# V of the attention layer computed by a Strassen product at the end of the gMLP layer

## The chip, the cores and the metric

The kernel runs on one core of a Trainium2 chip. A core has TensorE (PE, matrix products; its weight loads are shown as PEld), VectorE (DVE), ScalarE (ACT), GpSimd (POOL) and SyncE (SP), which issues the transfers between DRAM and the on-chip memory. Each engine takes its instructions in order. The metric is the device time of one execution in microseconds; of several runs the median is given.

## The reference, cut to what matters

Two layers act on x, 2048 tokens of width 1024, in float32. Layer A is a gated MLP over groups of 128 tokens. Layer B is attention in chunks of 64 tokens, each over itself and the 8 chunks before; its K and V come from the output x1 of layer A.

```
h  = rms_norm(x, a_norm_g)
u, v, z = split(h @ w_in, 3)                  # 1024 -> 3 x 2048
x1 = x + (gelu(u) * mix(layer_norm(gelu(v))) * silu(z)) @ w_out
k, v = split(rms_norm(x1, g_kv) @ w_kv, 2)    # 1024 -> 2 x 1024, the V of this case
q, z = split(rms_norm(x1, b_norm_g) @ w_qz, 2)
o  = softmax(q k^T + rel_bias over 9 chunks) v, 16 heads of 64
out = rms_norm(x1 + (o * silu(z)) @ wb_out, final_norm_g)
```

V is a product of 2048 x 1024 (normalized rows of x1) and 1024 x 1024 (the second half of w_kv, its rows scaled by g_kv). It is needed head by head, beside Q, K and the gate z.

## The kernel before, in words

Every float32 product is made of three products of rounded halves: a number is split into hi (a copy in the rounded type fp32r) and lo (the rest), and mm3 (lines 96 to 98) adds hi·hi, hi·lo and lo·hi in PSUM. A split is a copy on ACT and a subtraction on DVE (lines 255 and 258, in layer B 176 and 177).

**Layer A** is one sequence of steps. Six input stages n = 0 to 5 and the output stage "o" are each a product by Strassen's scheme in Winograd's form: both operands are cut in 2 x 2 blocks, and seven products of sums of blocks take the place of eight. The seven are the phases, in the order PH = (1, 2, 6, 5, 7, 4, 3), and each has 8 steps j, one for a pair of row blocks of 128 tokens. In stage o a step is 24 matmuls of 128 x 512 (Po). For each phase the weights' sums T are loaded, combined on GpSimd in pieces of 256 columns (line 264) and split. The row operands of stage o are So: prep_out loads blocks of the gated rows from DRAM (A<-ytd, line 796, a ring of four buffers; the first blocks stay in sc), adds or subtracts them (line 821 and its neighbours on DVE, line 264 on GpSimd in s2_of) and splits them. evict adds each PSUM result to the partial sums of its block, and done_out adds the residual x (xr) and stores x1 into x1d.

run_steps runs act of step s (its matmuls) and before it prep of step s + 3 (LOOK = 3); at(s, f) puts other work at a step, among it the weight loads and load_scaled. load_scaled loads 512 KB of weights (line 161), scales them by g on GpSimd (line 165) and stores the scaled ones for later tiles (line 168). All transfers are issued by SP in the order in which they stand. The framework's scheduler orders the instructions of each engine within what the data allow; that order is then fixed.

Steps of stage o are counted from nin, its first step. Weights for layer B are scaled at nin + 26, 28 and 30 (K, Q, Z of the first pair of heads) and nin + 32 and 34 (V of the first two pairs, raw_bv). At nin + 51 the rows of the first token tile are begun.

**Layer B** takes four tiles t of 512 tokens, each with eight pairs of heads p. norm_transpose (lines 118 to 157) makes the operands of a tile once: it loads x1 rows (bx_b), normalizes them (statistics on DVE, a power on GpSimd, line 115, a scaling on DVE), transposes them on TensorE (tr_b, line 145), and splits the result into hh_b and hl_b (lines 150 and 151). The first tile's is done at the end of stage o, the others' inside the projections.

The attention of a pair (t, p) has 8 slots: score (matmul s, the row maximum and bias on DVE at line 1067, the exponential on ACT at 1074, the scaling on GpSimd at 1078), flip (transposes tp, copies pt at 1098 to 1102) and value (pv, lines 1118 to 1125). Between them a generator yields the projections of the next pair as filler: Q and K with 8 yields each, V for two pairs at once with 16 yields of 6 matmuls of 128 x 256 (vp, proj_v), and the gate with 8 yields. Gates of two pairs are computed in the even pair. share fixes how many yields go into a pair, 32 before. proj_v splits V (lines 965 and 966) and stores it (vhd), since the next tile needs it as its previous 8 chunks. The output projection b4 (bo) stands between tiles.

Of the kernel before, what the change touches and what calls it, by code (L numbers as in the profile page):

```python
# [33 lines left out]
def trunk_kernel(  # L34
# [83 lines left out]
    def norm_transpose(name, src, wide, pool, tag, bufs):  # L118

        th = sh.tile([P, KD, T], F32R, tag="hh", name=f"hh_{name}")  # L120
        tl = sh.tile([P, KD, T], F32R, tag="hl", name=f"hl_{name}")

        xs = {}

        def norm(b):
            xt = pool.tile([P, D], F32, tag=tag, name=f"bx_{name}_{b}", bufs=bufs)
            nc.sync.dma_start(xt[:], src(b))
            r = inv_rms(xt, f"{name}_{b}")
            nc.vector.tensor_scalar(xt[:], xt[:], r[:], None, op0=ALU.mult)
            xs[b] = xt  # L130

        def block(b):
            if b not in xs:
                norm(b)
            xt = xs[b]
            if wide:
                pt = ptr.tile([P, KD, P], F32, tag="tr", name=f"tr_{name}_{b}")
                half = [pt[:, 0:4, :], pt[:, 4:8, :]]
            else:
                half = [  # L140
                    pmm.tile([P, 4, P], F32, tag="mm", name=f"tr_{name}_{b}_{h}")[:]
                    for h in range(2)
                ]
            for k in range(KD):
                tpose(half[k // 4][:, k % 4, :], xt[:, k * P : (k + 1) * P], ident[:])
            for h in range(2):
                ks = slice(h * 4, h * 4 + 4)
                oh = th[:, ks, b * P : (b + 1) * P]
                ol = tl[:, ks, b * P : (b + 1) * P]
                nc.scalar.copy(oh, half[h])  # L150
                nc.vector.tensor_tensor(ol, half[h], oh.bitcast(F32), op=ALU.subtract)
            if b + 2 < TB:
                norm(b + 2)

        for b in range(2):
            norm(b)
        return [(th[:, k, :], tl[:, k, :]) for k in range(KD)], block
# [29 lines left out]
    def v_source(t, pp, half):  # L187
        name = f"bv{int(t)}_{pp}_{half}"
        if t:
            return wvv[pp][:, half, :], name  # L190
        g = kg[:, half * 4 : half * 4 + 4, :]
        return w_vv[pp, :, half, :], name, g, wvv[pp][:, half, :]

    xT = {}

    def b1(t, *where):
        xT[t], block = norm_transpose(
            f"b{t}", lambda b: x1d[t][b * P : (b + 1) * P, :], t == 0, *where
        )
        return block  # L200
# [8 lines left out]
    with ExitStack() as actx:  # L209
# [598 lines left out]
        def prep_out(ph, j):  # L808
# [10 lines left out]
            elif ph == 7:  # L819
                v, b = y_load(0, 0, j, ph), y_load(1, 0, j, ph)  # L820
                tv(v, v, b, op=sub)
# [566 lines left out]
```

## Time and profile before

| | us |
|---|---|
| three runs, lowest, median, highest | 2738.63, 2742.27, 2744.74 |
| the profiled execution, its span | 2739.6 |
| layer A before stage o | 0 to 1069.9 |
| stage o | 1069.9 to 1404.1 |
| layer B | 1404.4 to the end |

The profiled execution's own time is its span; the medians of the runs lie 2.7 us above it. In the profile's tables, a row of a stretch of time gives for each engine its busy time and the count of instructions (x), then the clock granted to TensorE (1.00 is full) and the DMA share and rate. In a row of the timeline stand start, duration, engine, line, operation and tiles; a bracket at its end tells how long the engine had been idle, and what it waited for. A group's row gives, after the bar, total busy time and the mean in ns of one, and then the idle time before its members. Names lose their numbers: Po stands for all Po tiles.

### The profile page before, as it was taken

The page shows a single profiled execution, that of the slowest core. Times are in us where ns is not written, and L with a number is a line of the kernel's source. Part 1 is how long each engine was busy: PE and PEld are TensorE (multiplying, and loading weights), DVE is VectorE, ACT ScalarE, POOL GpSimd, SP SyncE. Part 2 cuts the span into 40 slices and gives each one's busy share as a digit, 9 for nine tenths or more (in the row PEclk, how much of TensorE's full clock was granted, in tenths as well). Part 3 has the DMA queues.
Part 4 walks back from the last instruction along what each step waited for, and adds up shares of the span by engine and source line. Part 5 has one row for each costly group of instructions (what it writes and reads, how often), then busy time and mean ns, then how long its engine had stood idle before and what let it go on. Part 6 is the DMA issues. An engine that isn't in the chain of part 4 may idle for free.

```text
span 2739.6 us, 40113 instructions
## 1 busy us (share of the span) xinstructions
PE 2673.4 (98%) x14176; PEld 2271.7 (83%) x14176; DVE 1918.0 (70%) x3211; ACT 1275.2 (47%) x2244; POOL 756.7 (28%) x951
## 2 busy tenths in 40 slices
PE   8899999999999999999999999999999999999997
PEld 6788888888888888777878888899988999889996
DVE  5556566756667566566767666877788777787777
ACT  5423243443433434232235554566655666556663
POOL 4611133241232423733024530211112112021111
PEclk9999999999999999999999999999999999999998
DMA  7799998986877868758766665455455444453331
GB/s 277 265 326 330 325 332 308 321 306 235 312 262 256 306 234 320 258 198 282 255 212 233 214 198 167 161 154 153 150 169 166 150 152 150 153 164 115 118 111 70
DMA packets 209191, 607.17 MB, mean 222 GB/s; under 512 B 24288, under 2 KB 24288, under 8 KB 208992
## 3 DMA queue, kind: packets, MB, share of 16 engines
q1 hardware_dynamic: 208992, 604.62, 64.3%
q8 instruction: 113, 1.85, 0.3%
q14 instruction: 86, 0.70, 0.1%
HBM read 466.11 MB, written 127.93 MB: 217 GB/s over the span
## 4 chain that ended last, share of the span: by engine, by line
PE 44%; DVE 7%; DMA 5%; POOL 2%; issue 1%; ACT 1%; SPq 0%; DVEq 0%; POOLq 0%; ACTq 0%
PE pj L96 5%; PE pj L97 5%; PE pj L98 5%; PE s L1059 4%; PE tp L1098 4%; PE pv L1125 4%; PE vp L98 2%; PE vp L96 2%; PE vp L97 2%; DMA A<-ytd 2%; PE bo L96 2%; PE bo L98 2%; PE bo L97 2%; PE Po L98 1%; PE Po L97 1%
## 5 line engine op out<-in xcount | busy, mean ns | idle before, releaser
L96 PE MATMUL P<-T,S 128*128 128x512 f32 x1248 | 496.3, 398 | 2.5 <-ACT S L255 2.1
L98 PE MATMUL P<-T,S 128*128 128x512 f32 x1248 | 490.6, 393 | 0.0
L97 PE MATMUL P<-T,S 128*128 128x512 f32 x1248 | 489.3, 392 | 1.1 <-DVE T L258 1.1
L1078 POOL TENSOR_SCALAR pr<-pr,sl 128x640 f32<-128x640 f32 (+4 forms) x256 | 200.2, 782 | 766.7 <-DVE sl L1077 678.6
L1074 ACT ACTIVATE pr<-pr,nm 128x640 f32<-128x640 f32 (+4 forms) x256 | 195.6, 764 | 274.8 <-DVE nm L1067 274.4
L96 PE MATMUL pj<-hh_b,wh_b 128*128 128x512 f32 x768 | 311.9, 406 | 0.7 <-ACT hh_b L150 0.7
L97 PE MATMUL pj<-hl_b,wh_b 128*128 128x512 f32 x768 | 302.6, 394 | 0.0
L98 PE MATMUL pj<-hh_b,wl_b 128*128 128x512 f32 x768 | 301.4, 392 | 0.0
L98 PEld LDWEIGHTS P<-T,S 128*128 128x128 f32 x1248 | 235.4, 189 | 50.1
L96 PEld LDWEIGHTS P<-T,S 128*128 128x128 f32 x1248 | 235.7, 189 | 45.1 <-ACT S L255 2.3
L97 PEld LDWEIGHTS P<-T,S 128*128 128x128 f32 x1248 | 235.7, 189 | 44.0 <-DVE T L258 1.3
L1102 DVE TENSOR_TENSOR pt<-tp,pt 128x640 fp32r<-128x640 f32 (+4 forms) x256 | 188.8, 737 | 59.0 <-ACT pt L1101 56.4
L1067 DVE CUSTOM_DVE_ANT_0 pr<-s,bias 128x640 f32<-128x640 f32 (+4 forms) x256 | 188.2, 735 | 44.6 <-PE s L1059 40.3
L98 PEld LDWEIGHTS pj<-hh_b,wl_b 128*128 128x128 f32 x768 | 144.5, 188 | 33.3
L1098 PE MATMUL tp<-ident,pr 128*128 128x128 f32 x1120 | 165.0, 273 | 4.6 <-DVE pt L1102 3.9
L1101 ACT CAST pt<-tp 128x640 fp32r<-128x640 f32 (+4 forms) x256 | 159.1, 621 | 21.1 <-PE tp L1098 15.5
L1098 PEld LDWEIGHTS tp<-ident,pr 128*128 128x128 f32 x1120 | 134.8, 140 | 32.3 <-issue 5.9
L96 PEld LDWEIGHTS pj<-hh_b,wh_b 128*128 128x128 f32 x768 | 144.9, 189 | 19.7 <-ACT hh_b L150 0.9
L97 PEld LDWEIGHTS pj<-hl_b,wh_b 128*128 128x128 f32 x768 | 145.3, 189 | 17.4
L96 PE MATMUL vp<-wh_bv,hh_b 128*128 128x256 f32 x512 | 148.3, 290 | 1.1 <-ACT hh_b L150 1.1
L98 PE MATMUL vp<-wh_bv,hl_b 128*128 128x256 f32 x512 | 145.6, 284 | 0.3
L97 PE MATMUL vp<-wl_bv,hh_b 128*128 128x256 f32 x512 | 145.1, 283 | 0.0
(216 smaller groups left out, 6103.9 us busy)
## 6 DMA issues: line engine op xcount, KB each, us to landing
S<-hsd SPq DMA_DIRECT2D x288, 512.0 KB, 5.0
rw<-in_w_a SPq DMA_DIRECT2D x108, 512.0 KB, 5.7
raw_b<-wk SPq DMA_DIRECT2D x75, 512.0 KB, 3.8
A<-ytd SPq DMA_DIRECT2D x72, 512.0 KB, 5.3
hsd<-S SPq DMA_DIRECT2D x56, 512.0 KB, 3.7
rwo<-in_w_out SPq DMA_DIRECT2D x40, 512.0 KB, 4.9
bias<-reld SPq DMA_DIRECT2D x64, 320.0 KB, 3.4
raw_bo<-in_wb_out SPq DMA_DIRECT2D x36, 512.0 KB, 3.9
```

Of the source, the lines that this page charges most:

```text
L96: mm(ps, lh, rh, start=first, stop=False)
L97: mm(ps, lh, rl, start=False, stop=False)
L98: mm(ps, ll, rh, start=False, stop=last)
L1059: mm(ps[:, sg, :w], q[:, qb * P : (qb + 1) * P], kx[:, koff + sg * w : koff + (sg + 1) * w], start=i == 0, stop=i == 1,)
L1067: nc.vector.tensor_tensor_reduce(out=pr[:, c0:].rearrange("p (a b) -> p a b", a=nseg), in0=ps[:, :nseg, :w], in1=bias[:, c0:].rearrange("p ...
L1074: nc.scalar.activation(pr[:, c0:], pr[:, c0:], AF.Exp, scale=-1.0, bias=nm[:], accum_out=sl[:])
L1078: nc.gpsimd.tensor_scalar(pr[:, c0:], pr[:, c0:], sl[:], 1.0, op0=ALU.mult, op1=ALU.mult)
L1098: tpose(tp[:, b, :], pr[:, b * P : (b + 1) * P], ident[:])
L1101: nc.scalar.copy(oh, tp[:, b0:5, :])
L1102: nc.vector.tensor_tensor(pt[:, 1, b0 + qq : 5 + qq, cs], tp[:, b0:5, :], oh.bitcast(F32), op=ALU.subtract)
L1125: mm(po[:, 0, :], keys(i), pt[:, j, i, :], start=(t == 0 and j == 0 and i == blocks[0]), stop=(j == 1 and i == blocks[-1]),)
```

## The change

A new stage "v" stands behind stage o in the sequence of steps: the same seven phases with 8 steps, each of 12 matmuls of 128 x 512 (Pv). Layer B then only loads V.

- The 16 row blocks of x1 are normalized once (row_norm: ACT squares and sums, GpSimd takes the power and scales), transposed (row_flip: eight transposes into tn, a copy on ACT) and stored transposed in xTd, in runs of 128 tokens. The odd blocks' are placed in the last phase of stage o, the even ones' in the first one and a half phases of stage v.
- prep_v loads halves of these blocks back (ring A, four buffers), and joins them on GpSimd in pieces. A step's result becomes V: done_vo splits it (hi on ACT, lo on GpSimd) and stores it in vhd.
- The eight quarters of V's weights are scaled at nin + 20 to nin + 41, every third step, and K, Q, Z of the first pair at nin + 43 to 47.
- norm_transpose becomes transposed: four loads of xTd per tile, each split by ACT and DVE.
- The subtraction of stage o's phase 3 goes from DVE to GpSimd pieces.
- In layer B proj_v is gone, project loads V from vhd (112 loads of 256 KB), and the gate is computed one pair ahead in every pair; share is 24 instead of 32.

```diff
-    def norm_transpose(name, src, wide, pool, tag, bufs):
-    ...
+    def transposed(t, pool, tag, bufs):
+        ...
+        def piece(i):
+            if i not in raws:
+                load(i)
+            ks = slice(2 * i, 2 * i + 2)
+            nc.scalar.copy(th[:, ks, :], raws[i][:])
+            nc.vector.tensor_tensor(
+                tl[:, ks, :], raws[i][:], th[:, ks, :].bitcast(F32), op=ALU.subtract
+            )
...
-        steps += [(n, ph, j) for n in (2, 3, 4, 5, "o") for ph in PH for j in range(NJ)]
+        steps += [(n, ph, j) for n in (2, 3, 4, 5, "o", "v") for ph in PH for j in range(NJ)]
...
-                v = sc[j]
-                tv(v, y_load(0, 1, j, ph), v, op=sub)
+                v, a = sc[j], y_load(0, 1, j, ph)
+                for g in range(2):
+                    pieces(v[:, g], a[:, g], v[:, g], sub)
...
+        for i, (r, c, q) in enumerate(wvs):
+            at(nin + 20 + 3 * i, lambda ...: load_scaled(w_vv[r, c, q], ..., wvs[r, c, q][:]))
+        for c in range(3):
+            at(nin + 43 + 2 * c, lambda c=c: load_scaled(*kqz_source(0, 0, c)))
+        def row_norm(blk):
+            xt = nxp[0].tile([P, D], F32, tag="bx", name=f"bx{blk}", bufs=2)
+            nc.sync.dma_start(xt[:], x1d[t][b * P : (b + 1) * P, :])
+            ...
+            nc.scalar.activation(..., xt[:], AF.Square, scale=1.0 / 32, accum_out=r[:])
+            nc.vector.tensor_scalar(r[:], r[:], EPS, None, op0=add)
+            nc.gpsimd.tensor_tensor(r[:], r[:], mhalf[:], op=ALU.pow)
+            nc.gpsimd.tensor_scalar(xt[:], xt[:], r[:], 1.0, op0=mul, op1=mul)
+        def row_flip(blk):
+            for k in range(KD):
+                tpose(pt[:, k, :], xt[:, k * P : k * P + P], ident[:])
+            xo = nxp[0].tile([P, KD, P], F32, tag="xv", name=f"xo{blk}", bufs=2)
+            nc.scalar.copy(xo[:], pt[:])
+            nc.sync.dma_start(xTd[t][:, :, b * P : b * P + P], xo[:])
+        def prep_v(ph, j):
+            ...
+            elif ph == 5:
+                v, b = x_half(1, 0, j, ph), x_half(1, 1, j, ph)
+                pieces(v, v, b, add)
+            elif ph == 7:
+                v, b = x_half(0, 0, j, ph), x_half(1, 0, j, ph)
+                pieces(v, v, b, sub)
+            elif ph == 4:
+                v = x_half(1, 1, j, ph)
+            else:
+                v = sc[j][1]
+                pieces(v, v, sc[j][0], sub)
+        def s2_of_v(j):
+            a, b = x_half(1, 0, j, 0), x_half(1, 1, j, 0)
+            pieces(a, a, b, add)
+            pieces(sc[j][0], a, sc[j][0], sub)
+        def done_vo(n, r, c, j, t):
+            vo = nxp[0].tile([P, 4, 4, 64], F32R, tag="xv", name=f"vo{blk}_{c}", bufs=2)
+            ...
+        for j in range(NJ):
+            for blk, s_ in ((2 * j + 1, nin + 48 + j), (2 * j, nv + 1 + 3 * j // 2)):
+                at(s_, lambda blk=blk: row_norm(blk))
+                at(s_ + 1, lambda blk=blk: row_flip(blk))
+            at(nv + 9 + j, lambda j=j: s2_of_v(j))
...
-            def proj_v(pp):
-            ...
+            if p % 2 == 0:
+                for b in range(0 if t > 0 else 4, 8):
+                    vv = sb.tile([P, 4, P], F32R, tag="V", name=f"V{t}_{pp}_{b}", bufs=14)
+                    nc.sync.dma_start(..., vhd[TB * t + b - 4][pp // 2][:, pp % 2, :])
...
-                if p % 2 == 0:
-                    yield from gate(t, p)
-                    yield from gate(t, p + 1)
+                yield from gate(t, p + 1)
...
-                return 32 * i // 16
-            return 34 * i // 16 if t + 1 < NT else 7 * i // 16
+                return 24 * i // 16
+            return 27 * i // 16 if t + 1 < NT else 7 * i // 16
```

Where the order of instructions moves, three places show it. The first is GpSimd's order at the end of stage o, before the change (do is the last residual add, rr_b the powers of the tile's row blocks, raw_b the scaled weights of the second pair):

```order
L845 TENSOR_TENSOR do_7_11203<-do_7_11203,xr15_1_11206 128x512
L115 TENSOR_TENSOR rr_b0_0_11673<-rr_b0_0_11673,mhalf_133 128x1
L115 TENSOR_TENSOR rr_b0_1_11685<-rr_b0_1_11685,mhalf_133 128x1
L115 TENSOR_TENSOR rr_b0_2_11788<-rr_b0_2_11788,mhalf_133 128x1
L115 TENSOR_TENSOR rr_b0_3_11843<-rr_b0_3_11843,mhalf_133 128x1
L165 TENSOR_TENSOR raw_b0_1_1_12206<-raw_b0_1_1_12206,bg_136 128x1024
```

And GpSimd's order in phases 2 and 6 of stage v after it (A0 joins an even block's two halves, sv takes it from the first block and, two rows on, from that block's second half for phase 3; rn and bx normalize a row block; vo is the lower half of a result):

```order
L243 TENSOR_TENSOR A0_10_1_12450<-A0_10_1_12450,A0_11_1_12452 128x256 x2
L243 TENSOR_TENSOR sv1_12019<-A0_10_1_12450,sv1_12019 128x256 x2
L243 TENSOR_TENSOR sv0_11962<-sv0_11962 128x256 x2
L243 TENSOR_TENSOR sv1_12019<-sv1_12019 128x256 x2
L895 TENSOR_TENSOR rn12_12461<-rn12_12461,mhalf_161 128x1
L896 TENSOR_SCALAR bx12_12458<-bx12_12458,rn12_12461 128x1024
L963 TENSOR_TENSOR vo1_0_12406<-cv_0_12404,vo1_0_12406 128x4x128
L963 TENSOR_TENSOR vo3_0_12446<-cv_1_12444,vo3_0_12446 128x4x128
L243 TENSOR_TENSOR A0_10_2_12488<-A0_10_2_12488,A0_11_2_12490 128x256 x2
L243 TENSOR_TENSOR sv2_12075<-A0_10_2_12488,sv2_12075 128x256 x2
L243 TENSOR_TENSOR sv2_12075<-sv2_12075 128x256 x2
L895 TENSOR_TENSOR rn14_12510<-rn14_12510,mhalf_161 128x1
```

Four single powers stood there; now the scalings, the sums for phase 6, those for phase 3 and the halves of V take turns in one queue.

The second place is TensorE at the end of stage o, before (Po is stage o's product, tr_b the transposes, pj and vp the first projections of layer B):

```order
L98 MATMUL Po_3_7_11893<-To_3_30_11426,So3_7_1_11765 128x512
L145 MATMUL tr_b0_3_11923<-ident_128,bx_b0_3_11836 128x128 x8
L96 MATMUL pj0_0_1_11960<-hh_b0_11664,wh_b1_0_1_11956 128x512
L96 MATMUL pj0_0_0_12003<-hh_b0_11664,wh_b1_0_0_11999 128x512
L96 MATMUL vp0_0_0_12048<-wh_bv1_0_0_12038,hh_b0_11664 128x256
```

And after, the end of stage o and that of stage v (tn are the transposes of a row block, Pv the products of stage v):

```order
L102 MATMUL Po_3_7_12047<-To_3_30_11477,So3_7_1_11908 128x512
L903 MATMUL tn15_12039<-ident_156,bx15_12037 128x128 x8
L100 MATMUL Pv_1_0_12093<-Tv_1_hh_11967,Sv1_0_11964 128x512
...
L102 MATMUL Pv_3_7_13670<-Tv_3_10_13425,Sv3_7_13624 128x512
L100 MATMUL pj0_0_1_13722<-hh_b0_13475,wh_b1_0_1_13718 128x512
L101 MATMUL pj0_0_1_13722<-hl_b0_13476,wh_b1_0_1_13718 128x512
```

The last tile's transposes and the first V block no longer stand between the two layers; stage v does.

The third place is SP in phase 7 of stage o, before (raw_bv are V's weights, A7 the rows of a step, wvv the store of the scaled weights):

```order
L161 DMA raw_bv0_0_0_10865<-in_w_vv 128x1024
L796 DMA A7_00_2_10854<-ytd0_0_2_247 128x1024
L796 DMA A7_10_2_10856<-ytd1_0_2_263 128x1024
L168 DMA wvv0_72<-raw_bv0_0_0_10865 128x1024
L796 DMA A7_00_3_10899<-ytd0_0_3_248 128x1024
L796 DMA A7_10_3_10901<-ytd1_0_3_264 128x1024
L161 DMA raw_bv0_0_1_10957<-in_w_vv 128x1024
```

And after (wvs is the store of the scaled quarter):

```order
L149 DMA raw_bv100_10897<-in_w_vv 128x1024
L780 DMA A7_00_1_10844<-ytd0_0_1_274 128x1024
L780 DMA A7_10_1_10846<-ytd1_0_1_290 128x1024
L156 DMA wvs1_0_0_76<-raw_bv100_10897 128x1024
L149 DMA raw_bv101_11034<-in_w_vv 128x1024
L780 DMA A7_00_2_10886<-ytd0_0_2_275 128x1024
L780 DMA A7_10_2_10888<-ytd1_0_2_291 128x1024
L156 DMA wvs1_0_1_77<-raw_bv101_11034 128x1024
```

The pattern is the same, a store of scaled weights between the row loads, with more of them in the stage as a whole.

More of the change, by code (lines that the diff above doesn't have):

```diff
@@ L60, in trunk_kernel @@
     wk3 = [dram.tile([P, 3, KD * P], F32, name=f"wk3_{p}") for p in range(NPAIR)]
-    wvv = [dram.tile([P, 2, 1024], F32, name=f"wvv{p}") for p in range(NPAIR // 2)]
+    wvs = {
+        (r, c, q): dram.tile([P, 1024], F32, name=f"wvs{r}_{c}_{q}")
+        for r in range(2) for c in range(2) for q in range(2)
+    }
+    xTd = [dram.tile([P, KD, T], F32, name=f"xTd{t}") for t in range(NT)]
     khd = [
@@ L66, in trunk_kernel @@
     vhd = [
-        [dram.tile([4, P, T], F32, name=f"vhd{t}_{p}") for p in range(NPAIR // 2)]
-        for t in range(NT - 1)
+        [dram.tile([P, 2, 512], F32, name=f"vhd{b}_{c}") for c in range(2)]
+        for b in range(S // P)
     ]
@@ L116, in inv_rms_of @@
         return r
-    def norm_transpose(name, src, wide, pool, tag, bufs):
[L120 to L157, printed above, removed]
@@ new lines, in transposed, with load @@
+    def transposed(t, pool, tag, bufs):
+        th = sh.tile([P, KD, T], F32R, tag="hh", name=f"hh_b{t}")
+        tl = sh.tile([P, KD, T], F32R, tag="hl", name=f"hl_b{t}")
+        raws = {}
+        def load(i):
+            raws[i] = pool.tile([P, 2, T], F32, tag=tag, name=f"bx_b{t}_{i}", bufs=bufs)
+            nc.sync.dma_start(raws[i][:], xTd[t][:, 2 * i : 2 * i + 2, :])
+        def piece(i):
[6 more added lines that the diff above has]
+            )
+            if i + 2 < 4:
+                load(i + 2)
+        for i in range(2):
+            load(i)
+        return [(th[:, k, :], tl[:, k, :]) for k in range(KD)], piece
@@ L185, in kqz_source @@
         return w_kqz[p, :, c, :], name, (bg if c else kg)[:, :, :], wk3[p][:, c, :]
[L187 to L192, printed above, removed]
     xT = {}
     def b1(t, *where):
[L197 to L200, printed above, removed]
+        xT[t], piece = transposed(t, *where)
+        return piece
     with ExitStack() as actx:
@@ L897, in trunk_kernel @@
         flush(1 << 30)
-        blocks[0](3)
+        nx.close()
         px.close()
@@ L986, in project @@
             if block:
-                yield from values()
+                for i in range(4):
+                    block(i)
+                    if i:
+                        yield
             for acc in one(t, p, 1):
@@ L1015, in project @@
                 kt[t, p, hd] = kx
-            if p % 2 == 0 and not block:
-                yield from values()
         def gate(t, p):
```

167 lines of the change are left out of this document (105 added, 62 removed).

## The prediction

> **What bounds the kernel now.** I read the page first, for engine shares and for the chain that ended last.
>
> ```profile
> span 2739.6 us, 40113 instructions
> PE 2673.4 (98%) x14176; PEld 2271.7 (83%) x14176; DVE 1918.0 (70%) x3211; ACT 1275.2 (47%) x2244; POOL 756.7 (28%) x951
> ```
>
> TensorE is busy 98% of the span, so TensorE time that is really taken out is gained, unless something else is late in its place. But a share says nothing of stages. The table by stretches of time does: stage o as a whole, four stretches in it, its end, and one of layer B (columns: us, then busy us and count of PE, PEld, DVE, ACT, POOL, granted clock, DMA share, GB/s).
>
> ```profile
> 1069.90:1404.10 334.20, 319.78 (x1382) 260.81 (x1381) 217.52 (x280) 97.81 (x152) 123.81 (x121) 0.97 0.69 243
> 1240.00:1250.00 10.00, 10.00 (x46) 8.29 (x45) 3.67 (x5) 1.14 (x2) 6.15 (x8) 1.00 0.90 342
> 1260.00:1280.00 20.00, 17.26 (x70) 13.24 (x70) 12.13 (x15) 7.22 (x10) 3.54 (x2) 0.96 0.82 285
> 1280.00:1300.00 20.00, 18.96 (x80) 15.23 (x80) 13.90 (x19) 3.32 (x6) 4.73 (x3) 0.96 0.85 297
> 1320.00:1340.00 20.00, 20.00 (x90) 16.57 (x89) 7.33 (x11) 4.25 (x7) 1.28 (x1) 1.00 0.94 326
> 1380.00:1400.00 20.00, 16.03 (x69) 13.18 (x68) 12.19 (x25) 2.75 (x5) 1.48 (x2) 0.83 0.30 93
> 2120.00:2220.00 100.00, 100.00 (x670) 91.99 (x669) 76.39 (x154) 63.39 (x118) 19.28 (x33) 1.00 0.49 152
> ```
>
> An undisturbed 20 us holds 90 matmuls of 512 columns. Stage o reaches that only in part, with DMA at 285 to 297 GB/s in two poor stretches and the best 10 us at 342; layer B runs without a gap, at 152 GB/s. So the change takes work out of a stretch that is purely bound by TensorE and puts a new stage behind one where memory traffic, SP and the vector engines are already late. The list of waits of TensorE says what is late there (total us, times, longest):
>
> ```profile
> PE Po L96 <- ACT So L255: 5.2, 2, 3.1
> PE Po L98 <- DVE So L258: 5.2, 5, 2.1
> PE tr_b L145 <- DVE hl_b L151: 4.0, 1, 4.0
> PE tr_b L145 <- DVE mv_b L109: 3.5, 1, 3.5
> ```
>
> The row operands So come late twice over, and the transposes for layer B wait at its door.
>
> **The change part by part.** *V out of layer B.* The groups show 512 matmuls on each of three lines, 1536 in all; a duration is not a price, since matmuls overlap. The price is the distance of starts, from the timeline: 16 distances in one V block, and 75 in stage o.
>
> ```profile
> L96 PE MATMUL vp<-wh_bv,hh_b 128*128 128x256 f32 x512 | 148.3, 290 | 1.1 <-ACT hh_b L150 1.1
> 1990.84 0.28 PE L96 MATMUL vp<-wh_bv,hh_b 128*128 128x256 f32 x1
> 1992.75 0.28 PE L97 MATMUL vp<-wl_bv,hh_b 128*128 128x256 f32 x1
> 1339.85 0.39 PE L96 MATMUL Po<-To_hh,So 128*128 128x512 f32 x1
> 1356.85 0.39 PE L96 MATMUL Po<-To,So 128*128 128x512 f32 x1
> ```
>
> 1.91 us / 16 = 0.1194, times 1536 = 183.4 us off. Stage v has 7 phases x 8 steps x 12 = 672 matmuls of 512 columns; 17.00 / 75 = 0.2267, times 672 = 152.3 us on. The transposes stay 16 groups of eight, at another place: nothing. Net on TensorE: **-31.1 us**. The loads of V (112 of 256 KB for 48 stores and 48 loads) go into layer B's 152 GB/s: nothing.
>
> *The door to layer B.* The row of 1380 to 1400 has 69 instructions, 16 of them transposes (two groups, about 1.6 us): 53 matmuls where (20.0 - 1.6) / 0.2267 = 81 would fit, so 28 x 0.2267 = 6.3 us are lost, the 4.0 us wait and the 0.83 clock behind it. In its place stands a load of finished rows and a split inside phase 3 of v, where nothing waits for it. With the 3.5 us wait of a later tile: **-9.8 us**. That stalls move elsewhere is costed where they go.
>
> *Stage o, more on its queue.* SP issues in order, and a store of a scaled weight waits there for GpSimd while the next rows A queue behind it:
>
> ```profile
> 1265.11 4.77 SPq L796 DMA_DIRECT2D A<-ytd  x2
> 1273.12 0.32 SPq L168 DMA_DIRECT2D wvv<-raw_bv  x1
> 1268.30 1.23 DVE L821 TENSOR_TENSOR A<-A,A 128x1024 f32<-128x1024 f32 x1 [3.23 <-DMA A<-ytd]
> ```
>
> Around the two such weights of phase 7, the stretch 1260 to 1300 loses 20 + 10 matmuls, 6.8 us. Before, stage o has five of these weights, after it has eleven, one in three steps instead of one in two; phases 5 and 7 hold about as many as before, the rest falls where one A or none is loaded per step. I take half of 6.8 again, 3 us. The add of phase 3 goes from VectorE (1.23) to four GpSimd pieces (about 3.4, below), which also have eight new row blocks to scale there, and each block's eight transposes stand in TensorE's order and can wait for it: 5 us, 0.6 per block. Together **+8** (from -4, the VectorE time freed, to +18, one longest So wait of 3.1 us for each of the six added weights).
>
> *Stage v, first three phases.* GpSimd gets here what one step needs before the next. From the first even row block to the last input of phase 6 its order holds 8 row blocks (a power and a scaling of 1024 columns), 64 pieces of 256 columns (16 for the weights of phase 6, 32 for the row sums, 16 that belong to phase 3 but stand behind each row) and 8 lower halves of V. None of these runs on before's GpSimd in just this form; the nearest rows:
>
> ```profile
> L264 POOL TENSOR_TENSOR ch<-rw,ch x96: 722/739/1808, 98.7 to 948.0; 128x256 f32<-128x256 f32 x96
> L264 POOL TENSOR_TENSOR A<-A,A 128x256 f32<-128x256 f32 x32 | 29.5, 951 | 53.4 <-DMA A<-ytd 53.4
> L115 POOL TENSOR_TENSOR rr_b<-rr_b,mhalf x16: 548/555/1008, 1374.0 to 2338.8; 128x1 f32<-128x1 f32 x16
> L1078 POOL TENSOR_SCALAR pr<-pr,sl 128x640 f32<-128x640 f32 x192 | 159.9, 833 | 701.9 <-DVE sl L1077 615.0 <-PE pv L1125 65.2 <-PE pj L97 11.9
> L654 POOL TENSOR_TENSOR z<-z,m 128x512 f32<-128x512 f32 x32 | 41.9, 1309 | 197.2 <-DVE z L653 197.2
> ```
>
> A piece costs 0.74 undisturbed and 0.95 on average in stage o; I take 0.84, halfway. A row block costs 0.66 (0.55 to 1.0) + 0.833 x 1024 / 640 = 2.0. A lower half costs 1.31. Sum: 8 x 2.0 + 64 x 0.84 + 8 x 1.31 = 80 us. It starts about 3 us into v (the first even row needs a buffer that the last odd row frees), and the last split and step follow with 4 us: phase 6 ends 87 to 89 us into v. TensorE needs 24 steps x 2.72 + 8 groups of transposes x 0.8 = 72. So **+16** (pieces at 0.74: +10, and +6 where the rows start early; at 0.95: +23). The spread of the same 256-column piece, 722 to 1808 ns, is what I rest the halfway value on.
>
> The Trainium skill ("SBUF — State Buffer", section "SBUF: two separate sides") says that VectorE operations with two SBUF inputs and GpSimd operations that read SBUF take one shared port pair by turns, each holding it for its whole instruction. The spread in the row agrees. By that rule a piece that waits half a split of 0.80 each time would cost 1.14, an estimate, and phase 6 would end 19 us later still: by the rule 2767, by the row what I forecast.
>
> *Stage v, phases 5 and 7.* Each step loads two half rows into a ring of four buffers, two pieces join them, and ACT and VectorE split the result before the buffers come free. The rows:
>
> ```profile
> L255 ACT CAST So<-A 128x512 fp32r<-128x512 f32 x64 | 37.3, 618 | 103.7 <-DVE A L821 42.1 <-DMA A<-ytd 25.2 <-PE Po L98 22.4
> L258 DVE TENSOR_TENSOR So<-A,So 128x512 fp32r<-128x512 f32 x64 | 50.8, 801 | 4.4 <-ACT So L255 4.4
> A<-ytd SPq DMA_DIRECT2D x72, 512.0 KB, 5.3
> xr<-in_x SPq DMA_DIRECT2D x32, 256.0 KB, 4.5
> Vh<-vhd SPq DMA_DIRECT2D x48, 256.0 KB, 4.0
> ```
>
> 4.0 (the shortest load of 256 KB) + 2 x 0.84 + 0.62 + 0.80 = 7.1 us for two steps, where TensorE needs 2 x 2.72 = 5.44. In stage o the same ring had steps twice as long. (7.1 - 5.44) / 2 x 16 steps = 13, less the lead of a step: **+12** (4 with the cover of a full lead in each phase, 45 if a load takes 8 us). Phases 4 and 3, with one load or none: **+3**. Stage v together +31, 13 to 71.
>
> A cross-check by bytes: v moves 18.9 MB of rows back, 16.8 of V out, 8.4 for the even rows, 9.4 of weights and 2.1 for layer B, 55.6 MB. Over 152 + 7 + 31 = 190 us that is 292 GB/s, as in stage o's poor stretches. Without stalls it would be 349, above the best 10 us of the trace.
>
> *Layer B with a shorter pair.* One pair of heads, 36.3 us, and what VectorE loses:
>
> ```profile
> 2000.00:2036.30 36.30, 36.30 (x217) 31.89 (x217) 28.30 (x50) 21.87 (x39) 3.75 (x6) 1.00 0.62 200
> L966 DVE TENSOR_TENSOR V<-vp,V 128x128 fp32r<-128x128 f32 x128 | 36.0, 284 | 5.1 <-ACT V L965 4.1
> L177 DVE TENSOR_TENSOR wl_bv<-raw_bv,wh_bv 128x1024 fp32r<-128x1024 f32 x32 | 40.6, 1269 | 0.9 <-ACT wh_bv L176 0.9
> PE tp L1098 <- DVE pt L1102: 3.9, 4, 2.2
> ```
>
> A pair falls to 36.3 - 183.4 / 32 = 30.6 us, VectorE's part to 28.3 - (36.0 + 40.6) / 32 = 25.9: from 78 to 85%. The softmax between scores and transposes is as long as it was, with 24 steps of projection as its cover for 32. I take 0.3 us per pair, 28 pairs: **+8** (0 to 25).
>
> **Sum:** -31.1 - 9.8 + 8 + 31 + 8 = +6.1 us on the profiled 2739.6, 2745.7. The median of the runs is 2742.27 (2738.63 to 2744.74), 2.7 above the span, so **2748.4 us**.
>
> **The rivals.** *A, stage v stays bound by TensorE.* Pieces at 0.74, the order's three-step lead covers the ring, and layer B and stage o lose half of what I take: -40.9 + 4 + 9 + 4 = -24, **2718**. For it: layer B shows that this code keeps TensorE at 1.00 where cover suffices. Against: v would last 168 us and move 331 GB/s all through, what 1320 to 1340 reaches for 20 us. It decides if phase 6 ends less than 80 us into v.
>
> *B, the short rows bind v.* The transposed rows are stored and read back in runs of 512 bytes. The trace has nothing like it:
>
> ```profile
> DMA packets 209191, 607.17 MB, mean 222 GB/s; under 512 B 24288, under 2 KB 24288, under 8 KB 208992
> ```
>
> Nothing lies between 512 bytes and 2 KB. From A's 512 KB in 5.3 us to xr's 256 KB in rows half as long in 4.5, one transfer's rate falls to 0.59. If 512-byte rows run at 0.59 of 326 GB/s, 192, the 23.1 MB in them (18.9 read back, 4.2 stored for the even rows) take 120 us and the other 32.5 MB 100: v lasts 220, not 190, **2778**. It decides if those loads land after 7 us or more. The Trainium skill ("DMA: Bandwidth & Descriptors", "Specifications") gives 512 bytes as the least transfer at line rate, and ("Why small descriptors are slow (HBM only)") some three cycles per packet besides. By it, an estimate, 16 of 19 cycles would be left, the two sums would be 84 + 100 us, below my 190, and this rival would be worth nothing. No row here shows it.
>
> *C, layer B gains less.* VectorE at 85% makes each pair lose one wait of transposes for pt, 3.9 / 4 = 1.0 us: 28 for my 8, **2768**. Against: today's 3.9 us are four waits in 256. It decides if TensorE's waits on pt in B exceed 20 us.
>
> **How the numbers follow.** My case 0.48, with a range of its own of 2728 to 2772 (v 13 to 50, the rest at its middle): 0.22 of it slower, 0.15 within 0.2% (5.5 us, about what a measurement of this kernel can tell from no change), 0.11 faster. A 0.26, faster. B 0.17 and C 0.09, slower. Faster 0.37, same 0.15, slower 0.48. The range must reach into A and to B: 2708 (A with nothing lost in stage o and B) to 2790.
>
> **What would show it.** Right: no vp and tr_b rows; TensorE's start-to-start in v at 0.227; phase 6 of v ends 85 to 92 us after its first Pv; TensorE waits there for Sv, behind GpSimd and A; pairs of layer B near 31 us with VectorE at 85%. Wrong: v under 170 us with no waits on Sv (then A), loads from xTd over 7 us and SP full (B), or waits on pt and nm in layer B above 20 us (C).

## The result, and the profile after

The changed kernel takes 2820.8 us (median of 4 runs, 2814.6 to 2822.6) where the kernel before takes 2741.8 beside it: 1.0285 times as long, 95% interval 1.0269 to 1.0301. The forecast was 2748.4 with a range of 2708 to 2790: slower was right as a direction, the size was not, and the time lies outside the range. The profiled execution has a span of 2817.9 us against 2739.6, so 78.3 us are to be found. Of e7 below, one execution took 5381 us where its three others took 2808 to 2815; its time is the median of the three, and its stretches are left blank.

First the page. TensorE has 1536 - 672 = 864 fewer matmuls, as forecast, and yet it is busy 8 us longer (2681.5 for 2673.4) and idle 70 us longer (136.4 for 66.2):

```profile
span 2817.9 us, 38956 instructions
PE 2681.5 (95%) x13312; PEld 2212.4 (79%) x13312; DVE 1926.2 (68%) x3081; ACT 1299.4 (46%) x2218; POOL 943.2 (33%) x1143
```

The stretches of the program follow from counting Po and Pv matmuls in the timeline (24 and 12 a step). "Forecast" puts the terms of the sum where they belong:

| us of the span | before | forecast | after | after - forecast |
|---|---|---|---|---|
| layer A up to stage o | 1069.9 | 1069.9 | 1074.2 | +4 |
| stage o | 334.4 | 339 | 358.5 | +19 |
| stage v: phases 1, 2, 6 | | 88 | 103.2 | +15 |
| stage v: phases 5, 7 | | 55.5 | 64.5 | +9 |
| stage v: phases 4, 3 | | 46.5 | 43.7 | -3 |
| behind the last Po or Pv | 1335.2 | 1146 | 1172.9 | +27 |

The first row is no cost of the change: the same stretch lasts from 1065.9 to 1080.8 us in the kernels below, whose code there is the same. All other rows but phases 4 and 3 are late. The table by stretches shows them (columns as before): stage o's phase 3 before the change, the same after it, then v's phases 1, 2, 6, then 5 and 7, then 4 and 3, and 100 us of layer B:

```profile
1351.40:1404.30 52.90, 48.93 (x217) 40.32 (x216) 39.05 (x71) 13.32 (x20) 3.42 (x4) 0.94 0.45 151
1364.60:1432.80 68.20, 54.61 (x250) 44.37 (x249) 35.91 (x51) 30.62 (x47) 40.68 (x39) 0.90 0.96 310
1433.60:1473.10 39.50, 30.73 (x131) 24.68 (x129) 13.78 (x24) 16.80 (x25) 18.69 (x24) 0.87 0.78 254
1473.10:1508.60 35.50, 28.48 (x130) 22.84 (x129) 13.54 (x21) 14.35 (x22) 31.00 (x38) 0.90 0.69 208
1508.60:1536.80 28.20, 24.13 (x97) 18.71 (x96) 12.54 (x14) 6.13 (x10) 25.87 (x30) 0.94 0.67 212
1536.80:1601.30 64.50, 50.00 (x194) 37.35 (x193) 32.97 (x44) 18.13 (x27) 45.20 (x51) 0.95 0.72 227
1601.30:1645.00 43.70, 43.70 (x194) 35.88 (x193) 35.30 (x42) 23.47 (x36) 23.60 (x16) 1.00 0.87 299
2300.00:2400.00 100.00, 99.85 (x592) 85.68 (x589) 81.03 (x157) 65.71 (x116) 22.07 (x39) 1.00 0.49 147
```

Three things are to be seen. Only the last two phases of v run at TensorE's own pace (8 steps in 21.8 us). Stage o's phase 3, which had DMA to spare before (a share of 0.45), now has a DMA share of 0.96. And where TensorE waits, the granted clock is below 1: in the v rows up to phase 7 TensorE idles 34.4 us (39.5 - 30.73, and so on), but v lasts 52.7 us longer than its 152.3 + 6.4 us of matmuls and transposes. The other 18 us are matmuls and transposes that follow one another more slowly, with no wait in between.

The list of TensorE's waits from stage o to the start of layer B (total us, times, longest) names other pairs than the forecast did, which looked for Sv behind GpSimd (tn are the transposes of a row block bx; xv and yv are partial sums, to which VectorE adds a finished product, line 346):

```profile
PE tn L903 <- POOL bx L896: 26.1, 10, 10.0
PE s L1138 <- DMA Qh<-Qh: 13.1, 1, 13.1
PE Po L102 <- DVE So L237: 12.1, 9, 3.6
PE Pv L100 <- DVE yv L346: 9.3, 6, 3.0
PE Po L100 <- ACT So L234: 9.0, 3, 3.1
PE Pv L100 <- DVE xv L346: 5.2, 3, 2.8
```

Of the 26.1 us for transposes, 10.3 stand in stage o's phase 3 and 15.8 in v's phases 1 and 2, where they are all of TensorE's idle time. The waits for xv and yv stand in phases 6, 5 and 7, and Sv is behind them all the same: VectorE's additions stand in its order behind splits whose operands are late. In phases 5 and 7 VectorE waits 27.9 us for ScalarE's half of the split, and one such wait hands itself on so:

```profile
DVE Sv L237 <- ACT Sv L234: 27.9, 14, 4.5
1544.56 0.99 DVE L237 TENSOR_TENSOR Sv<-A,Sv 128x512 fp32r<-128x512 f32 x1 [2.20 <-ACT Sv L234]
1545.47 0.68 DVE L346 TENSOR_TENSOR xv<-Pv,xv 128x512 f32<-128x512 f32 x1
1546.30 0.47 PE L100 MATMUL Pv<-Tv,Sv 128*128 128x512 f32 x1 [1.15 <-DVE xv L346]
```

The longest wait of transposes, 10.0 us, stands in stage o's phase 3. The timeline of GpSimd and TensorE around it:

```profile
1380.34 15.80 POOL L243 TENSOR_TENSOR sc<-A,sc 128x256 f32<-128x256 f32 x16
1396.10 0.99 POOL L895 TENSOR_TENSOR rn<-rn,mhalf 128x1 f32<-128x1 f32 x1
1398.37 1.97 PE L903 MATMUL tn<-ident,bx 128*128 128x128 f32 x8 [10.03 <-POOL bx L896]
```

Sixteen pieces of later steps' subtractions stood ahead of one row block's power and scaling, and that block's transposes stood in TensorE's order ahead of products whose operands were ready.

At the door of layer B (SyncE, GpSimd and TensorE) V's last result waits behind a weight's scaling on GpSimd, its store and V's loads hold SP, and Q's transfer is issued behind them. The last line is the stretch behind the wait, with a granted clock of 0.52:

```profile
1657.67 2.07 POOL L153 TENSOR_TENSOR raw_b<-raw_b,bg 128x1024 f32<-128x1024 f32 x1 [4.96 <-DMA raw_b<-in_w_kqz]
1659.70 1.27 POOL L963 TENSOR_TENSOR vo<-yv,vo 128x512 fp32r<-128x512 f32 x1
1661.00 0.32 SPq L966 DMA_DIRECT2D vhd<-vo  x1
1663.16 3.19 SPq L1058 DMA_DIRECT2D V<-vhd  x4
1666.46 0.52 SPq L1080 DMA_DIRECT2D Qh<-Qh  x1
1673.40 0.45 PE L1138 MATMUL s<-K,Qh 128*128 128x128 f32 x1 [13.07 <-DMA Qh<-Qh]
1673.40:1679.57 6.17, 6.17 (x18) 5.16 (x19) 2.33 (x6) 3.56 (x7) 0.00 (x0) 0.52 0.82 304
```

### The profile page after: what moved, and what is told of

Its sections match the earlier page's. It is cut to its first block, busy times and chain, and to the rows that moved or that the text cites. A ratio compares the mean times of both kernels' runs of the same rounds, so it can differ in the third digit from the quotient of the medians.

```text
span 2817.9 us, 38956 instructions
## 1 busy us (share of the span) xinstructions
PE 2681.5 (95%) x13312; PEld 2212.4 (79%) x13312; DVE 1926.2 (68%) x3081; ACT 1299.4 (46%) x2218; POOL 943.2 (33%) x1143
## 5 line engine op out<-in xcount | busy, mean ns | idle before, releaser
L1157 POOL TENSOR_SCALAR pr<-pr,sl 128x640 f32<-128x640 f32 (+4 forms) x256 | 208.6, 815 | 710.0 <-DVE sl L1156 651.8
L1146 DVE CUSTOM_DVE_ANT_0 pr<-s,bias 128x640 f32<-128x640 f32 (+4 forms) x256 | 188.0, 734 | 30.2 <-PE s L1138 25.9
L102 PEld LDWEIGHTS pj<-hh_b,wl_b 128*128 128x128 f32 x768 | 145.0, 189 | 29.5
L165 DVE TENSOR_TENSOR wl_b<-raw_b,wh_b 128x1024 fp32r<-128x1024 f32 x96 | 123.0, 1281 | 29.6 <-ACT wh_b L164 26.3
L1204 PE MATMUL pv<-pt,V 128*128 128x256 f32 x960 | 139.2, 285 | 0.0
L605 ACT ACTIVATE m<-mx,bsh 128x256 f32<-128x256 f32 x128 | 60.4, 473 | 160.0 <-PE mx L102 150.6
```

The lines of the kernel that those rows point to most:

```text
L102: mm(ps, ll, rh, start=False, stop=last)
L165: nc.vector.tensor_tensor(wl[:], raw[:], wh[:].bitcast(F32), op=ALU.subtract)
L605: nc.scalar.activation(m[:, :, c], px[:, i], AF.Identity, scale=0.5, bias=bsh[:, hh : hh + 1])
L1146: nc.vector.tensor_tensor_reduce(out=pr[:, c0:].rearrange("p (a b) -> p a b", a=nseg), in0=ps[:, :nseg, :w], in1=bias[:, c0:].rearrange("p ...
L1157: nc.gpsimd.tensor_scalar(pr[:, c0:], pr[:, c0:], sl[:], 1.0, op0=ALU.mult, op1=ALU.mult)
L1204: mm(po[:, 0, :], keys(i), pt[:, j, i, :], start=(t == 0 and j == 0 and i == blocks[0]), stop=(j == 1 and i == blocks[-1]),)
```

## The experiments

All are edits of the changed kernel, except where they name another. Theory 1: the rows go through too few buffers and too many queues, one behind another. Theory 2, the forecast's: GpSimd has too much to do before phase 6 ends. Theory 3: the runs of 512 bytes bind. Theory 4, formed after e6: SP's one queue (4b) or the bytes that it moves (4a).

Times are medians in us. The stretches are those of one profiled execution each, and they move where the code is the same, too: stage o's first six phases last from 286.4 to 296.1 us in these kernels. A few us in one stretch tell nothing by themselves.

| | time | stage o ph. 3 | v 1, 2, 6 | v 5, 7 | last Pv to first tp |
|---|---|---|---|---|---|
| changed kernel | 2820.8 | 68.2 | 103.2 | 64.5 | 35.9 |
| e1 rows ahead | 2809.6 | 65.2 | 100.4 | 63.3 | 31.3 |
| e2 GpSimd relieved | 2809.2 | 62.6 | 98.2 | 62.4 | 35.2 |
| e3 deep ring | 2808.9 | 68.8 | 99.3 | 55.0 | 35.0 |
| e4 V ring | 2815.2 | 70.9 | 99.4 | 64.4 | 36.0 |
| e5 = e1 + e2 + e3 | 2797.8 | 57.4 | 106.8 | 52.6 | 30.2 |
| e6 raw rows | 2803.5 | 55.1 | 104.1 | 62.3 | 30.1 |
| e7 long runs | 2811.5 | | | | |
| e8 door | 2811.2 | 70.9 | 104.4 | 61.8 | 29.5 |
| e9 GpSimd's V halves too | 2801.2 | 62.5 | 93.8 | 60.0 | 34.6 |
| e10 = e6 + e9 | 2785.5 | 44.5 | 97.8 | 61.4 | 27.3 |
| e11 sums early | 2819.0 | 67.2 | 98.7 | 62.2 | 36.0 |
| e12 all | 2783.2 | 60.0 | 89.7 | 54.5 | 23.6 |
| e13 = e10 + long runs | 2784.9 | 43.5 | 93.1 | 60.1 | 29.8 |
| e14 = e12, short runs | 2780.4 | 57.7 | 95.7 | 54.4 | 26.2 |
| e15 = e7 | 2814.3 | 68.2 | 100.0 | 60.5 | 33.7 |
| e16 = e10 + e3 | 2782.5 | 45.7 | 99.3 | 52.5 | 32.9 |
| e17 = e14, store by ACT | 2787.6 | 62.5 | 102.2 | 43.6 | 23.2 |
| e18 = e17, row rings | 2783.0 | 63.1 | 105.7 | 43.6 | 22.7 |

TensorE's own time is 43.5 us in stage o's phase 3 (some 50 with its transposes), 65.3 + 6.4 in v's phases 1, 2, 6, and 43.5 in 5 and 7.

**e1, rows ahead.**

```diff
+                at(s_ - 2, lambda blk=blk: row_load(blk))
                 at(s_, lambda blk=blk: row_norm(blk))
-tag="bx", name=f"bx{blk}", bufs=2
+tag="xv", name=f"bx{blk}", bufs=3
-            xo = nxp[0].tile([P, KD, P], F32, tag="xv", name=f"xo{blk}", bufs=2)
+            for h in range(2):
+                xo = nxp[0].tile([P, 4, P], F32, tag="xo", name=f"xo{blk}_{h}", bufs=2)
```

> Row blocks loaded two steps ahead into three buffers (shared with the V results), their transposed copies stored in two halves; same sums on every engine. Theory 1 (the row blocks go round two buffers, and a load, square, power, scaling and transposes of one pair last longer than the steps that TensorE has between its transposes): TensorE's wait of the transposes for the scaled rows, 26.1 us, falls under 10, stage o's phase 3 from 68.2 to about 58, phases 1 and 2 of v from 75 to about 62, the time by 15 to 25 us. Theory 2 (GpSimd has too much to do before phase 6 ends, as predicted) and theory 3 (transfers in runs of 512 bytes bind): within 5 us of the changed kernel.

11 us faster, less than theory 1 asked: the wait of the transposes stays at 23.2 us, of which 13.6 is one wait behind GpSimd's burst in stage o; phases 1 and 2 of v gain 9 us, and phase 6 gives 6 back.

**e2, GpSimd relieved.**

```diff
-                for g in range(2):
-                    pieces(v[:, g], a[:, g], v[:, g], sub)
+                tv(v, a, v, op=sub)
...
-                pieces(v, v, sc[j][0], sub)
+                tv(v, v, sc[j][0], op=sub)
```

> Phase 3's subtractions of stage o (32 pieces) and of stage v (16 pieces) on VectorE instead of GpSimd. Theory 2: GpSimd loses about 12 us of its work ahead of the end of phase 6 and about 27 us in phase 3 of stage o: 15 to 25 us faster, about half of it in v. Theory 1: phase 3 of stage o gains up to 8 us, where 16 pieces stand ahead of a row block's scaling, stage v nothing; up to 8 us faster. Theory 3: nothing.

12 us faster: 5.6 in stage o's phase 3 (theory 1 allowed 8), 5.0 in v's first three phases (theory 2 asked for 8 to 12). Neither theory explains it alone. With the burst gone, the same transposes still wait 8.7 us at once, now because SP issues the row's load 9 us after its buffer is free.

**e3, deep ring.**

```diff
-                v, b = x_half(1, 0, j, ph), x_half(1, 1, j, ph)
+                v, b = x_two(1, 0, 1, 1, j, ph)   # both halves in one [P, 2, 4, P] buffer of tag "A"
```

> The two half rows of a step in phases 5 and 7 (and of the row sums) share one buffer of the ring, which was half empty: the ring holds four steps, not two. Theory 1: phases 5 and 7 of v fall from 64.5 us to 44 to 50, the time by 15 to 20 us. Theory 2: the same pieces, under 5 us. Theory 3: the same transfers, under 5 us.

Phases 5 and 7 fall by 9.5 us, the time by 12, less than theory 1 asked (44 to 50 us, 15 to 20): the ring is real, and holds about half of these phases' excess of 21 us.

**e4, V ring, and e11, sums early.** `tag="bx" if r + c and j % 2 else "xv"` for vo; `at(nv + 5 + 3 * j // 2, ...)` for the row sums.

> In phases 7, 4 and 3 of stage v the V results use the row blocks' two idle buffers as well, four instead of two. Theory 1: the last stores of V come earlier, TensorE's 13.1 us wait for Qh at the start of layer B falls under 5, the time by 8 to 12 us. Theory 2 and theory 3: within 4 us of the changed kernel.

> The row sums for phase 6 are placed from the fifth step of v on, three for two steps, not from the ninth on, one a step: GpSimd's work and its loads start up to 11 us sooner. Theory 2: phase 6 ends earlier, 3 to 8 us. Theory 1 and 4: the loads stand ahead of row loads and stores in SP's queue and hold them up: 0 to 5 us slower.

e4's wait for Qh stays at 13.2 us: V's results wait for GpSimd and SP, not for a buffer. e11 gains 4.5 us in the first three phases, as theory 2 asked, and loses it elsewhere; the time is the changed kernel's within 2 us.

**e5, the three together.**

> The three edits that each gained 8 to 13 us together: rows loaded ahead, phase 3's subtractions on VectorE, the deep ring. Theory 1 (several queues that stand behind one another: each edit alone only hands the wait to the next queue): more than the three gains added, since stage o's phase 3 loses its one long stall (68.2 to 51-56) only when both SP's late load and GpSimd's burst are gone: 2770 to 2782. Theory 2 (GpSimd's amount of work): about the sum of e2 and e3, near 2797. Theory 3 (transfers of 512-byte runs): no better than the best single edit, 2800 to 2809.

2797.8, 23 us faster, less than the three gains added (35), and the time that theory 2 gave (near 2797). Theory 1's sign, a gain in stage o's phase 3 beyond the single ones, is hardly there: 57.4 us, where the gains of e1 and e2 added give 59.6 and the theory asked for 51 to 56. v's first three phases get longer, 106.8.

**e6, raw rows.** Normalization and transposes of the row blocks are left out; rows are stored as loaded.

```diff
-            nc.scalar.activation(..., AF.Square, ...)   # and the sum, power, scaling, transposes, copy
+            nc.sync.dma_start(xTd[t][:, :, b * P : b * P + P], xt[:].rearrange("p (a b) -> p a b", a=KD))
```

> Leaves out the normalization and the transposes of the row blocks: the rows of x1 are loaded and stored as they are (so V and layer B are computed from other numbers); every load and store stays, also those in runs of 512 bytes. Theory 1: stage o's phase 3 falls from 68.2 to about 45, v's first three phases from 103 to 70-75: 45 to 55 us faster, near 2770. Theory 2: GpSimd keeps 64 pieces and 8 halves, 64 us, and loses 16: 15 to 30 us faster in v, 10 in o. Theory 3: v's first three phases stay over 95; under 25 us faster.

This is where theory 1 fell as the whole story: stage o's phase 3 gains 13 us, but v's first three phases stay at 104.1 with no row work in them. Those are the signs of theory 3 (over 95, under 25 us faster), which the long runs below test. GpSimd in phase 6 of e6:

```profile
1485.07 1.73 POOL L951 TENSOR_TENSOR vo<-cv,vo 128x512 fp32r<-128x512 f32 x1
1486.76 1.41 POOL L243 TENSOR_TENSOR A<-A,A 128x256 f32<-128x256 f32 x2
1488.13 1.42 POOL L243 TENSOR_TENSOR sv<-A,sv 128x256 f32<-128x256 f32 x2
1489.51 1.43 POOL L243 TENSOR_TENSOR sv<-sv 128x256 f32<-128x256 f32 x2
1490.89 1.74 POOL L951 TENSOR_TENSOR vo<-cv,vo 128x512 fp32r<-128x512 f32 x1
```

Without a gap, 5.8 us for one step of 2.72. Here the forecast's mechanism is seen bare: six pieces and a half of V set the pace. The changed kernel has the same lots of 5.8 us in its phase 6, from 1516.8 to 1528.5.

**e9, GpSimd's V halves on VectorE too, and e10, with raw rows.** `nc.vector` for `nc.gpsimd` in done_vo, on top of e2.

> As e2 (both phase 3 subtractions on VectorE), and all lower halves of V on VectorE too: GpSimd is left with the row blocks, the weights' sums and the 32 pieces of the row sums, about 55 of the 80 us that the prediction counted before the end of phase 6. Theory 2 (GpSimd's amount sets the end of phase 6): v's first three phases, 98 us in e2, fall to 85 to 90. Theory 1 (the row blocks' chain through the queues): they stay within 4 us of e2. Theory 4 (SP's one queue and what it moves, whatever the engines do): they stay at 98 to 104.

> e6 (rows stored as they are, no normalization, no transposes) and e9 together: neither the rows' chain nor GpSimd's amount is left, every transfer is. If theories 1 and 2 between them hold the excess of v's first three phases, these fall from 104 us to 70 to 78 (65 is TensorE's own). Theory 4: they stay over 90.

e9 takes the first three phases to 93.8, short of theory 2's 85 to 90. e10 has neither the rows' work nor the pieces and halves that e9 takes off GpSimd, and stays at 97.8, as theory 4 said. Its phase 2 runs at TensorE's pace (21.8 us), phases 1 and 6 last 36.7 and 39.3. The stretch table of its phase 1, and of e13's:

```profile
1406.70:1443.40 36.70, 27.08 (x98) 19.28 (x97) 16.53 (x24) 9.03 (x14) 1.10 (x1) 0.91 1.03 324
```

```profile
1415.00:1447.60 32.60, 25.52 (x98) 18.15 (x97) 16.34 (x24) 9.03 (x14) 0.18 (x1) 0.95 0.98 347
```

The DMA engines are busy from end to end (shares of 1.03 and 0.98, counted by the packets that start in the stretch), at rates that the kernel before reached for 10 to 20 us at a time. What ScalarE's half of the split waits for in e10 differs between phase 1 (first line) and phase 6 (second):

```profile
ACT Sv L234 <- DMA sv<-xTd: 29.4, 7, 6.9
ACT Sv L234 <- POOL sv L243: 28.0, 8, 4.8
```

So the 15 us that phase 1 is late are transfers. Phase 6 waits for the row sums, which e10 leaves on GpSimd: GpSimd is busy 27.6 of 39.3 us there and waits 7.5 for loads. For phase 6, e10 does not tell theory 2 from theory 4.

**e7 and e15, e12, e13, e14: long runs.** The rows lie in DRAM block by block, so that stores run over 4096 bytes and half blocks over 2048.

```diff
-    xTd = [dram.tile([P, KD, T], F32, name=f"xTd{t}") for t in range(NT)]
+    xTd = [dram.tile([TB, P, KD, P], F32, name=f"xTd{t}") for t in range(NT)]
```

> The transposed rows lie in DRAM block by block, so that a store has runs of 4096 bytes and a half row block of 2048 instead of 512; layer B's 16 loads of a tile become 64 of a quarter, still in runs of 512. Theory 3: loads and stores of transposed rows land in two thirds of the time, phases 5 and 7 lose their excess, 20 us or more faster. Theories 1 and 2: loads land a little sooner, under 8 us faster.

> e7 again. Theory 3: v's first three phases under 95, phases 5 and 7 under 55. Theories 1, 2 and 4a: 98 to 104 and 60 to 65; the time 5 to 10 us below the changed kernel in both cases.

> Every mending together: e5, e7's long runs, e9's work moved to VectorE, and V's loads of the first pair behind Q and K. If the losses were separate, 24 + 8 + 6 + 6 us: 2775 to 2785. By theory 4 no better than e5, 2795 to 2800. Neither reaches the kernel before, 2741.

> e10 with the rows laid out block by block in DRAM: stores in runs of 4096 bytes, half blocks read in runs of 2048. Theory 3: v's first three phases fall from 98 to under 80, and the DMA share in phase 1 from 1.03 to under 0.9. Theory 4a (bytes and SP's order): they stay over 90, the rate in phase 1 near 324 GB/s.

> e12 without the long runs. Theory 3: v's first three phases go back from 90 to 98 or more, the time up by 8 to 15 us against e12. Theory 4a: within 5 us of e12.

e15 is e7 again. Long runs gain 9 and 7 us alone (2811.5, 2814.3), where theory 3 asked for 20; nothing beside the other mendings (e12 2783.2, e14 2780.4), and nothing in e13 against e10 (2784.9, 2785.5), though v's first three phases win 6 and 5 us there. Theory 3 is out as the main cause.

**e8, door.** V's loads of the first pair behind Q and K; V's lower halves in phases 4 and 3 on VectorE.

> At the start of layer B the loads of V are issued behind Q and K, and the lower halves of V in phases 4 and 3 are formed on VectorE, not on GpSimd. Theory 1: the wait of 13.1 us for Qh falls under 5, the first transposes of layer B start 8 to 14 us sooner after the last Pv (36 us now), the time by as much. Theory 2: under 4 us, since GpSimd has spare time there. Theory 3: the stores of V still have to land first, under 4 us.

The time falls by 9.6 us, as theory 1 said. Layer B's first transposes come 6.4 us sooner, and the wait for Qh is 8.5 us, not under 5. In the profiled execution the part from there to the end lasts 6 us longer (1143.2 for 1137.0), but that execution took 2823.8 us and the three others 2809.7 to 2812.0. e12, e14, e17 and e18 issue V's loads in the same order: 1147.3, 1138.1, 1139.0 and 1136.9. So what the door gains is not given back as a rule.

**e16, e17, e18: what is left.** The deep ring in e10; stores of the transposed rows from ScalarE's queue; and their copies in the ring of 25 partial sums, with four row buffers.

> e10 with e3's deep ring, which the row sums of phase 6 use too. Theory 1 (rings and queues, one behind another): phase 6 falls from 39 to 22-26, phases 5 and 7 from 61 to 52, v's first three phases to 78-84, the time by 15 to 25 us. Theory 4a (the bytes bind): v's first three phases stay over 90, what phase 6 gains phase 1 or 2 gives back.

> e14 with the stores of the transposed rows issued by ScalarE instead of SP. Theory 4b (SP's single queue): v's first three phases fall from 95.7 to under 88 and stage o's phase 3 from 57.7 to under 54, the time by 8 to 15 us against e14. Theory 4a (the bytes): within 5 us of e14, first three phases over 92. Neither comes within 20 us of the kernel before.

> e17 with the transposed copies in the ring of partial sums and four buffers for the row blocks. Theory 1 (rings and queues, one behind another): v's first three phases fall from 102 to 78-85, ScalarE's wait for the stores from 39.6 us to under 10, the time by 15 to 25 us, to 2763-2773; still slower than the kernel before. Theory 4a (the bytes): they stay over 92, the time within 6 us of e17.

e16: the ring is not what holds v's first three phases (99.3). In e17 phases 6, 5, 7, 4 and 3 run at TensorE's own 21.8 us each, where e14 still lost 11 us in 5 and 7. But phases 1 and 2 lose most of that again, 80.4 us for 72.0, stage o's phase 3 the rest, and the time is 7 us longer, not 8 to 15 shorter as theory 4b asked. It is not the stores themselves that held phases 5 and 7: e14 issues the last of them at 1485.1, and its phase 6 begins at 1490.8. Since e17 spends more time ahead of these phases, more can be ready for them; whether that is the reason was not tested. e18 does not shorten phases 1 and 2. Its table of phase 1, phase 2 and the rest:

```profile
1429.70:1476.10 46.40, 32.82 (x140) 26.68 (x137) 22.02 (x33) 21.22 (x36) 30.03 (x36) 0.81 0.99 332
1476.10:1513.10 37.00, 30.26 (x123) 24.80 (x122) 14.41 (x24) 13.96 (x25) 23.56 (x31) 0.82 0.69 208
1513.10:1622.30 109.20, 109.20 (x481) 89.79 (x480) 93.04 (x125) 47.91 (x73) 43.92 (x42) 1.00 0.84 271
```

In phase 1 the DMA engines are busy throughout again (0.99). SyncE's longest waits in e18 are loads that stand behind the stores of the rows that they read back (first line, from stage o's phase 3 to phase 2); 15.6 us of them are in phase 1, but only 2.8 in phase 2. There SP waits longest for V's lower halves on VectorE (second line) and for the weights' sums on GpSimd:

```profile
SPq L922 <- DMA xTd<-xo: 36.8, 14, 8.4
SPq L981 <- DVE vo L978: 10.4, 3, 7.2
SPq L262 <- POOL chv L243: 10.3, 2, 7.3
```

No version comes near the kernel before; the shortest, e14, is 1.0143 times as long (1.0123 to 1.0163), and e10, e12, e16 and e18 lie within 5 us of it. No version moves fewer bytes, so that rival is not tested by taking bytes away.

## Why the prediction was wrong

**TensorE's part was right.** The count of matmuls is the forecast's, the last phases of stage v run at the pace behind its 152.3 us, and the price of V off layer B holds: steady pairs of layer B take 31.2 us, where 30.6 plus 0.3 was forecast.

**"Stage v, first three phases: +16" failed in mechanism and size.** 103.2 us against 88. The forecast let GpSimd run through its 80 us of work without a wait, 3 us into v, and took the rows' transposes as free TensorE time. The amount was about right: GpSimd is busy 75.6 us in these phases. But in phases 1 and 2 it stands still for 25.5 us, until a late row block's sum of squares is there:

```profile
POOL rn L895 <- DVE rn L894: 25.5, 6, 7.3
```

Behind it stand that block's transposes, for which TensorE waits 15.8 us in these two phases. Only in phase 6 does GpSimd's work set the pace (25.87 of 28.2 us busy), as forecast. e9 shows that the pieces and halves taken off GpSimd held some 9 us. e6 and e10 show that without the rows' work the phases are no shorter (104.1 for 103.2, 97.8 for e9's 93.8): what e10 loses in phase 1 is transfers, and in phase 6 the rest of GpSimd's sums has a part. e10 moves 36.7 x 324 + 21.8 x 289 + 39.3 x 266 = 28.6 MB in these phases:

```profile
1443.40:1465.20 21.80, 21.80 (x98) 17.87 (x96) 13.77 (x18) 5.65 (x9) 18.11 (x20) 1.00 0.92 289
1465.20:1504.50 39.30, 29.13 (x98) 19.93 (x97) 25.87 (x34) 9.86 (x16) 27.61 (x30) 0.87 0.86 266
```

At 342 GB/s, the best 10 us before, that is 84 us, where TensorE needs 65 in e10. The forecast's cross-check averaged the bytes over all of v and saw 292 GB/s; they crowd into its beginning and into stage o's phase 3 (DMA share 0.96 for 0.45). What of the last 10 to 20 us is bytes, what is the order of stores and loads in one queue, and what is left of GpSimd's work stays open: e17 and e18 moved the loss between phases, took 4 and 1 us off the whole of v, and lost 5 in stage o's phase 3.

**"Stage o: +8" was mis-sized.** The stage lasts 19 us longer than the forecast has it, in two terms. Phase 3 makes 13 of them: its own 43.5 us, 8 groups of transposes at 0.8 and the forecast's 5 us for transposes that wait give 55, and it lasts 68.2, through a chain of queues that the forecast didn't follow: GpSimd's burst, SP's late load, ScalarE's Square behind a load. e2 and e1 each removed one link and left the other's wait; e5 removed both, 57.4; without rows and without the pieces on GpSimd (e10) the phase lasts 44.5. The first six phases make the other 6: 290.4 us for 281.5 before, where the six added weights were priced at 3. TensorE's waits for So are 18.0 us there, for 10.4 before. No version took these weights away, so that they are the cause is not shown.

**"In its place stands a load ..., where nothing waits for it" failed.** The door to layer B costs 13.1 us of wait and 3 us of slow clock behind it (6.17 us at 0.52), 16 of the 27 us that layer B is behind the forecast. I had looked at the rows' operands and not at V itself, which is stored, loaded, and stands ahead of Q in SP's queue. e12, e14, e17 and e18 take the wait to between 2.6 and 5.1 us. The rest lies in the first tile's first four pairs (105.1 us, where the next take 24.8 each) and in 0.3 us for each steady pair.

**The ring of phases 5 and 7 was right in kind**: 64.5 us for 55.5 forecast, 55.0 with twice the ring (e3). What holds the rest is not shown; e17 and e18 reach 43.6, behind longer phases 1 and 2.

**A factor was missing.** The forecast's own row of the door before showed 6.3 us lost for a wait of 4.0, and no other stall was priced that way. In v 34.4 us of idle time cost 52.7. The factor is no constant: the 13.1 us at the door cost 16.

**The rivals.** A (v bound by TensorE) was refuted by its own condition, phase 6 ending less than 80 us into v. B gave a time nearer the result, 2778, for a wrong reason: the loads in runs of 512 bytes land in 3.8 us, sooner than the 4.0 that I took,

```profile
A<-xTd SPq DMA_DIRECT2D x56, 256.0 KB, 3.8
```

and long runs gain nothing beside the other mendings. The Trainium skill ("DMA: Bandwidth & Descriptors", "Specifications") puts the least transfer at line rate at 512 bytes; the traces agree (3.8 us for 256 KB in runs of 512 bytes, 3.6 in runs of 2048 in e15). C was not it: TensorE's waits for pt in layer B fell to 0.8 us. The Trainium skill's port rule ("SBUF — State Buffer", "SBUF: two separate sides") would, by the forecast's estimate, have made a piece 1.14 us. In v's phase 6 they run at 0.71 (1.42 for two, above in e6), where VectorE is busy 12.54 of 28.20 us, and in stage o's burst at 0.99 (15.80 for 16), where it is busy 11.52 of 15.80. That a fuller VectorE is the reason was not tested. My 0.84 lies between the two, and the estimate of 1.14 above both.

## What to carry to other kernels

A stage that reads back what it has just written must be priced as a chain, from store to load to engine to store, beside the sum of each engine's work: here GpSimd's work was summed about right, but GpSimd stood still for 25.5 us in the middle of it. Bytes are to be counted for the phase in which they must move, not over the stage. And work taken out of a stretch that is bound by TensorE alone is worth its matmuls only if what takes its place runs as free of waits: here 31 us of matmuls were saved, and some 105 us were lost elsewhere (78.3 + 31.1, less the 4.3 of layer A).
